# Softmax normalized through the turning product, negated scores with their minimum, and gates of two pairs written together

## The chip, the cores and the metric

The kernel runs on one core of a Trainium2 chip. The metric is the device time of one execution in microseconds, the median of the runs; lower is better. The core has a matmul engine (TensorE, here PE), VectorE (DVE), ScalarE (ACT), GpSimd (POOL) and a queue that issues transfers (SP). Each engine works through its own instructions in the order in which they stand.

## What is computed

Two blocks follow each other on a sequence of 512 positions of width 1024. The first has two layers with feed-forward networks, of which the second holds a sparse attention with 8 heads (`dsa` in the kernel); the second block holds a gated delta rule and a forgetting attention with 16 heads of width 64 (`fox`). Of the reference, the two attentions matter here:

```python
def dsa_attention(q, k, v, qi, ki, wi):            # cut
    ...
        s = jnp.where(valid[:, :, None, None, :], s, -jnp.inf)
        p = jax.nn.softmax(s, axis=-1)
        o = jnp.einsum('btgrk,btkgd->btgrd', p, v_sel.astype(jnp.float32))
...
def forgetting_attention(q, k, v, cum):            # cut
    ...
        logits = jnp.einsum('bqhd,bkhd->bhqk', q_b, k)
        logits = logits + (c_b[..., :, None] - cum_k[..., None, :])
        q_pos = start + jnp.arange(Q_BLOCK)
        mask = key_pos[None, :] <= q_pos[:, None]
        p = jax.nn.softmax(jnp.where(mask, logits, -jnp.inf), axis=-1)
        return jnp.einsum('bhqk,bkhd->bqhd', p, v)
...
    o = forgetting_attention(q, k, v, cum).reshape(B, S, FOX_WIDTH)
    o = o * jax.nn.silu(z.astype(jnp.float32))
```

## The kernel before

Nearly all of the time goes into projections. A weight of 128x1024 is loaded as f32 (`raw`), cast to a high part `wh` on ACT (line 139) and a low part `wl` on DVE or GpSimd (line 140), and each product is made of three matmuls (lines 145 to 147) into a PSUM bank named `acc`, of which there are three. Scores go into two banks `sa`, turned probabilities into two banks `sb`.

**Both attentions** go by steps. In `dsa` a step is a head and a query block `i` of 128 rows: 8 heads times 4 blocks, of widths 128, 256, 384 and 512. In `fox` it is a pair of heads `p`, a head `a` of it and a block `i`: 8 times 2 times 4 = 64 steps of the same widths. A step has three parts, each issued one step after the last:

- `scores`: products into `sa`; one DVE instruction adds a bias, writes the sum to `x` (tile `p`) and its row maximum to `st`; a small DVE instruction makes the maximum negative (lines 897 and 1472); ACT takes the exponential with that as its bias and sums the row (898 and 1473); DVE takes the reciprocal (899 and 1474); `x` is multiplied by it, in `dsa` on ACT (900), in `fox` on DVE (1475).
- `turn`: each of the `i + 1` blocks of 128x128 in `x` is turned by a PE transpose with the identity (lines 907 and 1484), and ACT copies the bank to `pT` (909 and 1485).
- `values`: in `dsa` `i + 1` plain f32 matmuls of 128x128 (line 917); in `fox` once for each pair (line 1493).

Between these parts units of projection work are let in by a generator (`fill`): a unit is one set of three matmuls, or six in `v_units`. In `fox`, `pair_units(p + 1)` brings, while pair `p` is at work, the query and the key of the next pair, and by turns the values or the two gates `z` of two pairs. When a gate's projection ends, ACT applies Silu to its bank (line 1430) and then loads the table set that has exponential and logarithm again (line 126, kept in program order). Query and key are normalized seven units after their projection ends (`normed`): ACT logarithm and exponential (lines 173 and 174) and three DVE steps make `r`, GpSimd multiplies `x` by it (1398), and ACT and DVE cut it into halves (1410 to 1420).

The order in which instructions stand on each engine is not that of the text: a planner sets it when the program is built, from when it thinks each operand is ready. So an edit in one place can move instructions in others.

Of the kernel before, what the change touches and what calls it, by code (L numbers as in the profile page):

```python
# [12 lines left out]
AF = mybir.ActivationFunctionType  # L13
ALU = mybir.AluOpType
# [5 lines left out]
D, S, DFF, KT, P = 1024, 512, 2816, 8, 128  # L20
# [8 lines left out]
def f32(ap):  # L29
    return ap.bitcast(F32)  # L30
# [410 lines left out]
def c4(ap, c):  # L441
    return ap[:, c * P:(c + 1) * P]
# [275 lines left out]
DSA_SCALE = 128.0 ** -0.5  # L718
TAKEN = -3.0e38
# [64 lines left out]
def dsa(self, tables):  # L784
    nc, tc, A = self.nc, self.tc, self.A
    with tc.tile_pool(name="ds", bufs=1) as ds:
        def T(name, shape=(P, S), dtype=F32, bufs=None):
            return ds.tile(list(shape), dtype, name=name, bufs=bufs)
# [26 lines left out]
        ps = self.bank()  # L815
# [21 lines left out]
        pt = self.bank("sb")  # L837
# [17 lines left out]
        bias = [cneg]  # L855
        for i in range(1, 4):
            W = (i + 1) * P
            x = T(f"isc{i}", (P, W))

            for t in range(2):  # L860
# [3 lines left out]
                for a, ps in enumerate(pair):  # L864
                    hh = 2 * t + a
                    r = self.tmp()
# [19 lines left out]
        prob, pos = {}, {}  # L886
        ogh, ogl = T("ogh", (P, KT, S), F32R), T("ogl", (P, KT, S), F32R)

        def scores(h, i):
            W = (i + 1) * P  # L890
            ps = self.bank("sa")
            nc.tensor.matmul(ps[:, :W], c4(qT[h], i), kT[h // 4][:, :W], start=True, stop=True)
            x = T("p", bufs=3)[:, :W]
            st = T("st", (P, 4), bufs=4)
            nc.vector.tensor_tensor_reduce(x, ps[:, :W], bias[i], 1.0, TAKEN, op0=ALU.add, op1=ALU.max,
                                           accum_out=st[:, 0:1])
            nc.vector.tensor_scalar(st[:, 1:2], st[:, 0:1], -DSA_SCALE, None, op0=ALU.mult)
            nc.scalar.activation(x, x, AF.Exp, scale=DSA_SCALE, bias=st[:, 1:2], accum_out=st[:, 2:3])
            nc.vector.reciprocal(st[:, 3:4], st[:, 2:3])
            nc.scalar.activation(x, x, AF.Copy, scale=st[:, 3:4])  # L900
            prob[h, i] = x

        def turn(h, i):
            x, W = prob.pop((h, i)), (i + 1) * P
            pt = self.bank("sb")
            for j in range(i + 1):
                nc.tensor.transpose(c4(pt, j), c4(x, j), self.ident)
            pT = prob[h, i] = T("pT", bufs=3)
            nc.scalar.copy(pT[:, :W], pt[:, :W])

# [20 lines left out]
        for t in range(len(steps) + 3):  # L931
            if t < len(steps):
                while len(qT) <= steps[t][0]:
                    fill.run(1)
                scores(*steps[t])
                if t < 12:
                    for r in range(t * 16 // 12, (t + 1) * 16 // 12):
                        top(3, r)
            if t == 19:
                fill.add(self.out_units(feed, 2, [ogh[:, u] for u in range(4)], [ogl[:, u] for u in range(4)], one))  # L940
            fill.run(3 if t < 5 else 1 if t < 16 else 2)
            if 1 <= t <= len(steps):
                turn(*steps[t - 1])
            if t >= 2 and t - 2 < len(steps):
                values(*steps[t - 2])
# [400 lines left out]
def fox(self, feed, gate, tail):  # L1346
    nc, tc, A = self.nc, self.tc, self.A
    BF = dt.bfloat16
    with tc.tile_pool(name="fx", bufs=1) as fx, tc.tile_pool(name="fxd", bufs=1, space=bass.MemoryType.DRAM) as dr:
        def T(name, shape=(P, S), dtype=F32, bufs=None):  # L1350
            return fx.tile(list(shape), dtype, name=name, bufs=bufs)
# [13 lines left out]
        ps, ps_q, ps_k = [self.bank() for _ in range(3)]  # L1365
# [16 lines left out]
        qs, ks, vs, zs, og = {}, {}, {}, {}, []  # L1382

        def normed(name, dst, p, gain_col, sq_scale, eps, halves):
            def done(ps):
                x, sq, sh = T("x", bufs=2), self.tmp(), T("sqh", dtype=F32R, bufs=2)
                nc.scalar.activation(sq, ps, AF.Square, scale=sq_scale)
                nc.scalar.activation(x, ps, AF.Copy, scale=gain_col)
                nc.scalar.activation(sh, ps, AF.Square, scale=sq_scale)
                sl = T("sql", dtype=F32R, bufs=2)  # L1390
                nc.vector.tensor_sub(sl, sq, f32(sh))

                def stats():
                    pn = self.bank()
                    nc.tensor.matmul(pn, blk, sh, start=True, stop=False)
                    nc.tensor.matmul(pn, blk, sl, start=False, stop=True)
                    r = self.rstd_from(pn, T("r", bufs=2), eps)
                    nc.gpsimd.tensor_mul(x, x, r)  # L1398
                    dst[p] = halves(x)
                fill.later(7, stats)  # L1400
            return done
# [21 lines left out]
        def v_copy(p):  # L1423
            v = vs[p] = vs[p + 1] = T("v", (P, 4, 256), bufs=2)
            return lambda c2, ps: nc.scalar.copy(v[:, 2 * c2:2 * c2 + 2].rearrange("p c d -> p (c d)"), ps)

        def z_done(p):
            def done(ps):
                zs[p] = T("sz", bufs=2)
                nc.scalar.activation(zs[p], ps, AF.Silu)  # L1430
                self.log_exp()
            return done

        def q_done(p):
# [2 lines left out]
        def pair_units(p):  # L1437
            nb = T("ncb", (P, 2, S), bufs=2)
            nc.sync.dma_start(nb.rearrange("p h s -> p (h s)"),
                              cd[2 * p:2 * p + 2].rearrange("h s -> (h s)").rearrange("(o f) -> o f", o=1)  # L1440
                              .to_broadcast([P, 2 * S]))
            nbs[p] = nb
            k_done = normed("k", ks, p, self.prm("b_kn"), 0.125, None, k_halves)
            if p == 0:
                q_done(0)(ps_q)
                k_done(ps_k)
            else:
                if p > 1:
                    yield from self.project_units(feed, q_done(p))
                yield from self.project_units(feed, k_done)  # L1450
            if p % 2 == 0:
                yield from self.v_units(feed, v_copy(p))
            else:
                yield from self.project_units(feed, z_done(p - 1))
                yield from self.project_units(feed, z_done(p))
            if p == 0:
                yield from self.project_units(feed, q_done(1))

        nbs, prob, pTs = {}, {}, {}

        def scores(p, a, i):
            q, (k, kl) = qs[p][:, a], ks[p]
            W = (i + 1) * P
            ps = self.bank("sa")
            nc.tensor.matmul(ps[:, :W], c4(q, i), k[:, a, :W], start=True, stop=False)
            nc.tensor.matmul(ps[:, :W], c4(q, i), kl[:, a, :W], start=False, stop=False)
            nc.tensor.matmul(c4(ps, i), ib, mb, start=False, stop=True)
            x = T("p", bufs=3)[:, :W]
            st = T("st", (P, 4), bufs=4)
            nc.vector.tensor_tensor_reduce(x, ps[:, :W], nbs[p][:, a, :W], 1.0, TAKEN, op0=ALU.add, op1=ALU.max,  # L1470
                                           accum_out=st[:, 0:1])
            nc.vector.tensor_scalar(st[:, 1:2], st[:, 0:1], -1.0, None, op0=ALU.mult)
            nc.scalar.activation(x, x, AF.Exp, bias=st[:, 1:2], accum_out=st[:, 2:3])
            nc.vector.reciprocal(st[:, 3:4], st[:, 2:3])
            nc.vector.tensor_scalar(x, x, st[:, 3:4], None, op0=ALU.mult)
            prob[p, a, i] = x

        def turn(p, a, i):
            if i == 0:
                pTs[p, a] = T("pT", (P, 4, S), bufs=2)  # L1480
            x, W = prob.pop((p, a, i)), (i + 1) * P
            pt = self.bank("sb")
            for j in range(i + 1):
                nc.tensor.transpose(c4(pt, j), c4(x, j), self.ident)  # L1484
            nc.scalar.copy(pTs[p, a][:, :i + 1, i * P:(i + 1) * P], pt[:, :W].rearrange("p (j t) -> p j t", t=P))


# [17 lines left out]
        for t in range(len(steps) + 2):  # L1505
            if t < len(steps):
                p, a, i = steps[t]
# [246 lines left out]
```

## Time and profile before

| | us |
|---|---|
| median of 3 runs (2778.74 to 2782.1) | 2779.63 |
| profiled execution | 2783.07 |
| its span | 2781.3 |
| PE busy in it | 2684.0 |
| DVE busy | 1729.3 |
| ACT busy | 1194.4 |
| POOL busy | 240.4 |

The span runs from the first to the last instruction that the profile shows. The busy share is a mean over stages with different limits, so the stretches that hold the edited lines have to be read by themselves. A row of the timeline joins consecutive instructions of one line; its second number is the time from the start of the first to the end of the last. PE records overlap: the next starts before the last has drained, and the spacing of starts is what a record costs.

### The profile page before, as it was taken

To read this page: it belongs to the slowest core of one execution; us is meant where nothing else is said; L and a number is where in the kernel's file an instruction comes from. 1 tells how busy PE (TensorE), PEld (TensorE's weight loads), DVE (VectorE), ACT (ScalarE), POOL (GpSimd) and SP (SyncE) were. 2 spreads that over 40 slices of the span, in tenths; PEclk is the share of its full clock that TensorE was granted. 3 is DMA by queue.
4 is the path that set the end of the run, shared out by engine and by line. 5 is a ranking of instruction groups with operands and counts; after the bars stand their busy time and mean duration, and the time that the engine had idled before them with its cause. 6 is when DMAs were issued, how large, how long until landed. Compare 5 with 4: busy or idle time off the path is not lost. (4 is left out here: it accounts for less than half of the span.)

```text
span 2781.3 us, 38312 instructions
## 1 busy us (share of the span) xinstructions
PE 2684.0 (97%) x14903; PEld 2192.8 (79%) x14903; DVE 1729.3 (62%) x3065; ACT 1194.4 (43%) x2200; POOL 240.4 (9%) x224
## 2 busy tenths in 40 slices
PE   8999999999999999999899999988999999999998
PEld 6888878788888888887778888876777777777776
DVE  6454576764545644447956444478777777677776
ACT  4232254532323422224364222265655554577774
POOL 0000002000000000003410000021111111120001
PEclk9999999999999999999999999998999999999999
DMA  5343432243443432323213333223333333132221
GB/s 187 117 138 113 121 103 69 84 144 114 136 121 107 136 111 97 93 87 91 69 39 91 99 99 94 83 83 93 101 99 101 111 98 97 48 101 69 76 67 63
DMA packets 106709, 274.60 MB, mean 99 GB/s; under 512 B 35464, under 2 KB 39552, under 8 KB 106528
## 3 DMA queue, kind: packets, MB, share of 16 engines
q1 hardware_dynamic: 106528, 272.15, 32.6%
q8 instruction: 118, 1.93, 0.3%
q14 instruction: 63, 0.52, 0.1%
HBM read 267.79 MB, written 4.31 MB: 98 GB/s over the span
## 5 line engine op out<-in xcount | busy, mean ns | idle before, releaser
L145 PE MATMUL acc<-xh,wh 128*128 128x512 f32 (+2 forms) x2320 | 911.5, 393 | 18.1 <-ACT xh L186 8.4
L146 PE MATMUL acc<-xl,wh 128*128 128x512 f32 (+1 forms) x2320 | 903.9, 390 | 3.3 <-POOL xl L151 2.4
L139 ACT CAST wh<-raw 128x1024 fp32r<-128x1024 f32 (+3 forms) x430 | 439.0, 1021 | 1089.8 <-PE acc L146 716.1
L147 PE MATMUL acc<-xh,wl 128*128 128x512 f32 (+1 forms) x2320 | 899.7, 388 | 2.1 <-DVE wl L140 2.1
L140 DVE TENSOR_TENSOR wl<-raw,wh 128x1024 fp32r<-128x1024 f32 (+2 forms) x410 | 490.4, 1197 | 67.4 <-ACT wh L139 64.7
L145 PEld LDWEIGHTS acc<-xh,wh 128*128 128x128 f32 (+1 forms) x2320 | 437.0, 188 | 109.1 <-ACT xh L186 8.3
L146 PEld LDWEIGHTS acc<-xl,wh 128*128 128x128 f32 x2320 | 436.6, 188 | 92.2 <-issue 3.7
L147 PEld LDWEIGHTS acc<-xh,wl 128*128 128x128 f32 x2320 | 436.1, 188 | 92.6 <-DVE wl L140 4.0
L146 PE MATMUL acc<-al,wh 128*128 128x512 f32 (+1 forms) x720 | 278.2, 386 | 0.0
L147 PE MATMUL acc<-ah,wl 128*128 128x512 f32 (+1 forms) x720 | 277.8, 386 | 0.0
L145 PE MATMUL acc<-ah,wh 128*128 128x512 f32 (+1 forms) x720 | 277.4, 386 | 0.0
L249 DVE SCALAR_TENSOR_TENSOR h<-acc,h 128x512 f32<-128x512 f32 x128 | 88.4, 691 | 214.8 <-PE acc L147 214.4
L289 DVE TENSOR_TENSOR tmp<-acc,rstd 128x512 f32<-128x512 f32 x88 | 60.9, 691 | 239.0 <-PE acc L147 239.0
L287 DVE TENSOR_TENSOR tmp<-acc,rstd 128x512 f32<-128x512 f32 x88 | 60.8, 691 | 175.7 <-PE acc L147 175.6
L146 PEld LDWEIGHTS acc<-al,wh 128*128 128x128 f32 x720 | 135.2, 188 | 28.6 <-DVE al L151 0.8
L145 PEld LDWEIGHTS acc<-ah,wh 128*128 128x128 f32 x720 | 135.2, 188 | 28.2
L147 PEld LDWEIGHTS acc<-ah,wl 128*128 128x128 f32 x720 | 135.2, 188 | 28.0
L140 POOL TENSOR_TENSOR wl<-raw,wh 128x1024 fp32r<-128x1024 f32 (+1 forms) x20 | 47.8, 2390 | 872.5 <-ACT wh L139 861.7
L145 PE MATMUL acc<-ogh,wh 128*128 128x512 f32 (+1 forms) x256 | 105.0, 412 | 10.5 <-DVE h L1301 6.7
L147 PE MATMUL acc<-ogh,wl 128*128 128x512 f32 (+1 forms) x256 | 100.3, 392 | 0.0
L146 PE MATMUL acc<-ogl,wh 128*128 128x512 f32 (+1 forms) x256 | 100.0, 391 | 0.0
L150 ACT CAST ah<-tmp 128x512 fp32r<-128x512 f32 x88 | 54.8, 622 | 64.0 <-DVE tmp L290 64.0
(450 smaller groups left out, 3472.0 us busy)
## 6 DMA issues: line engine op xcount, KB each, us to landing
raw<-in_wi_dram SPq DMA_DIRECT2D x176, 512.0 KB
raw<-in_wo_dram SPq DMA_DIRECT2D x64, 512.0 KB
raw<-in_ada_w_dram SPq DMA_DIRECT2D x48, 512.0 KB
raw<-in_a_in_dram SPq DMA_DIRECT2D x48, 512.0 KB
raw<-in_b_in_dram SPq DMA_DIRECT2D x24, 512.0 KB
raw<-in_wo_dram SPq DMA_DIRECT2D x24, 384.0 KB
raw<-in_a_out_dram SPq DMA_DIRECT2D x16, 512.0 KB
big<-rd SPq DMA_DIRECT2D x13, 512.0 KB
```

The costliest lines, as they stand in the source:

```text
L139: nc.scalar.copy(wh[:, :n], raw[:, :n])
L140: self.lo_eng.tensor_tensor(wl[:, :n], raw[:, :n], f32(wh[:, :n]), op=ALU.subtract)
L145: nc.tensor.matmul(out, ah, bh, start=start, stop=False)
L146: nc.tensor.matmul(out, ah, bl, start=False, stop=False)
L147: nc.tensor.matmul(out, al, bh, start=False, stop=stop)
L150: self.nc.scalar.copy(hi, x)
L249: nc.vector.scalar_tensor_tensor(self.h[m], ps, scale(m), self.h[m], op0=ALU.mult, op1=ALU.add)
L287: nc.vector.tensor_mul(t, pg, rstd)
L289: nc.vector.tensor_mul(u, pu, rstd)
```

## The change

In both attentions the reducing instruction now multiplies by a negative number (-1, in `dsa` the negative scale) and takes the row minimum, which is the bias that the exponential wants; the exponential's scale is -1. The small multiplication is gone. The reciprocal no longer multiplies the probabilities: it multiplies the identity into a tile `dg` of 128x128 (three buffers), on ACT in `dsa` and on DVE in `fox`. The transposes become plain matmuls of the probabilities with `dg`, which turn and scale in one. The gates: the first of two is left in its bank until the second is projected, and both are then written after each other, with one call that loads the other table set. The tile `r` has one buffer in place of two.

```diff
@@ dsa: scores, turn
-            nc.vector.tensor_tensor_reduce(x, ps[:, :W], bias[i], 1.0, TAKEN, op0=ALU.add, op1=ALU.max,
+            nc.vector.tensor_tensor_reduce(x, ps[:, :W], bias[i], -DSA_SCALE, -TAKEN, op0=ALU.add, op1=ALU.min,
                                            accum_out=st[:, 0:1])
-            nc.vector.tensor_scalar(st[:, 1:2], st[:, 0:1], -DSA_SCALE, None, op0=ALU.mult)
-            nc.scalar.activation(x, x, AF.Exp, scale=DSA_SCALE, bias=st[:, 1:2], accum_out=st[:, 2:3])
+            nc.scalar.activation(x, x, AF.Exp, scale=-1.0, bias=st[:, 0:1], accum_out=st[:, 2:3])
             nc.vector.reciprocal(st[:, 3:4], st[:, 2:3])
-            nc.scalar.activation(x, x, AF.Copy, scale=st[:, 3:4])
-            prob[h, i] = x
+            dg = T("dg", (P, P), bufs=3)
+            nc.scalar.activation(dg, self.ident, AF.Copy, scale=st[:, 3:4])
+            prob[h, i] = x, dg
...
-                nc.tensor.transpose(c4(pt, j), c4(x, j), self.ident)
+                nc.tensor.matmul(c4(pt, j), c4(x, j), dg, start=True, stop=True)
@@ fox: normed, z_done
-                    r = self.rstd_from(pn, T("r", bufs=2), eps)
+                    r = self.rstd_from(pn, T("r"), eps)
...
-                zs[p] = T("sz", bufs=2)
-                nc.scalar.activation(zs[p], ps, AF.Silu)
-                self.log_exp()
+                zs[p] = ps
+                if p % 2:
+                    for q in (p - 1, p):
+                        ps, zs[q] = zs[q], T("sz", bufs=2)
+                        nc.scalar.activation(zs[q], ps, AF.Silu)
+                    self.log_exp()
@@ fox: scores, turn
-            nc.vector.tensor_tensor_reduce(x, ps[:, :W], nbs[p][:, a, :W], 1.0, TAKEN, op0=ALU.add, op1=ALU.max,
+            nc.vector.tensor_tensor_reduce(x, ps[:, :W], nbs[p][:, a, :W], -1.0, -TAKEN, op0=ALU.add, op1=ALU.min,
                                            accum_out=st[:, 0:1])
-            nc.vector.tensor_scalar(st[:, 1:2], st[:, 0:1], -1.0, None, op0=ALU.mult)
-            nc.scalar.activation(x, x, AF.Exp, bias=st[:, 1:2], accum_out=st[:, 2:3])
+            nc.scalar.activation(x, x, AF.Exp, scale=-1.0, bias=st[:, 0:1], accum_out=st[:, 2:3])
             nc.vector.reciprocal(st[:, 3:4], st[:, 2:3])
-            nc.vector.tensor_scalar(x, x, st[:, 3:4], None, op0=ALU.mult)
-            prob[p, a, i] = x
+            dg = T("dg", (P, P), bufs=3)
+            nc.vector.tensor_scalar(dg, self.ident, st[:, 3:4], None, op0=ALU.mult)
+            prob[p, a, i] = x, dg
...
-                nc.tensor.transpose(c4(pt, j), c4(x, j), self.ident)
+                nc.tensor.matmul(c4(pt, j), c4(x, j), dg, start=True, stop=True)
```

The planner gives a new order in places. On ACT, in `fox`, where the first of the two gates of pairs 2 and 3 stands (`sz` is the gate, `p` the probabilities, `ks` the key's halves), there stood before:

```order
L1473 ACTIVATE p_21148,st_21149<-p_21148,st_21149 128x256
L173 ACTIVATE r_21164<-acc_21161,eps0_79 128x512
L174 ACTIVATE r_21164<-r_21164,ln_a_87 128x512
L1430 ACT_TABLE_LOAD
L1430 ACTIVATE sz_21188<-acc_21125 128x512
L126 ACT_TABLE_LOAD
L1485 COPY pT_21191<-sb_21192 128x128
L1417 CAST ks_21172<-x_21095 64x512
L1419 CAST ks_21172<-x_21095 64x512
L1417 CAST ks_21172<-x_21095 64x512
L1419 CAST ks_21172<-x_21095 64x512
L1473 ACTIVATE p_21199,st_21200<-p_21199,st_21200 128x384
```

After the two rows of lines 173 and 174 there stand now:

```order
L139 CAST wh_21272<-raw_21271 128x1024
L1491 COPY pT_21187<-sb_21188 128x128
L1435 ACT_TABLE_LOAD
L1435 ACTIVATE sz_21248<-acc_21124 128x512
L1478 ACT_TABLE_LOAD
L1478 ACTIVATE p_21195,st_21196<-p_21195,st_21196 128x384
L1418 CAST ks_21171<-x_21094 64x512
L1420 CAST ks_21171<-x_21094 64x512
L1418 CAST ks_21171<-x_21094 64x512
L1420 CAST ks_21171<-x_21094 64x512
L1491 COPY pT_21187<-sb_21221 128x2x128
L1478 ACTIVATE p_21229,st_21230<-p_21229,st_21230 128x512
```

The first gate still stands by itself, the second a row further on; a weight cast and the 384-wide exponential moved ahead of the key's casts.

On ACT, in `fox`, at the 512-wide step that ends a pair, while values are projected, there stood before:

```order
L1485 COPY pT_21546<-sb_21586 128x2x128
L139 CAST wh_21645<-raw_21644 128x1024
L1425 COPY v_21445<-acc_21561 128x512
L1485 COPY pT_21546<-sb_21626 128x3x128
L139 CAST wh_21731<-raw_21730 128x1024
L1473 ACTIVATE p_21594,st_21595<-p_21594,st_21595 128x512
L1473 ACTIVATE p_21635,st_21636<-p_21635,st_21636 128x128
L1485 COPY pT_21546<-sb_21663 128x4x128
```

and now:

```order
L1491 COPY pT_21544<-sb_21584 128x2x128
L139 CAST wh_21643<-raw_21642 128x1024
L1478 ACTIVATE p_21592,st_21593<-p_21592,st_21593 128x512
L1426 COPY v_21443<-acc_21559 128x512
L1491 COPY pT_21544<-sb_21624 128x3x128
L139 CAST wh_21729<-raw_21728 128x1024
L1478 ACTIVATE p_21633,st_21634<-p_21633,st_21634 128x128
L1491 COPY pT_21544<-sb_21661 128x4x128
```

The 512-wide exponential moved ahead of the copy of `v`, a copy of `pT` and a weight cast.

On PE, in `fox`, at the change from pair 2 to pair 3 (lines 1465 to 1467 are the new pair's first scores, line 1484 turns the last pair's 384-wide step), there stood before:

```order
L147 MATMUL acc_21212<-xh7_104,wl_21121 128x512
L1465 MATMUL sa_21260<-ks_21172,qs_21084 128x128
L1466 MATMUL sa_21260<-kl_21173,qs_21084 128x128
L1467 LDWEIGHTS ib_19897
L1467 MATMUL sa_21260<-mb_19895,ib_19897 128x128
L145 MATMUL acc_21279<-xh0_97,wh_21207 128x512
L146 MATMUL acc_21279<-xl0_105,wh_21207 128x512
L147 MATMUL acc_21279<-xh0_97,wl_21208 128x512
L1484 MATMUL sb_21255<-ident_74,p_21199 128x128 x3
```

and now:

```order
L147 MATMUL acc_21208<-xh7_104,wl_21120 128x512
L1490 MATMUL sb_21253<-dg_21200,p_21195 128x128 x3
L1470 MATMUL sa_21258<-ks_21171,qs_21083 128x128
L1471 MATMUL sa_21258<-kl_21172,qs_21083 128x128
L1472 LDWEIGHTS ib_19897
L1472 MATMUL sa_21258<-mb_19895,ib_19897 128x128
L145 MATMUL acc_21277<-xh0_97,wh_21203 128x512
L146 MATMUL acc_21277<-xl0_105,wh_21203 128x512
L147 MATMUL acc_21277<-xh0_97,wl_21204 128x512
```

The turn moved ahead of the new pair's scores and of three projection matmuls.

## Rows read from the trace of the kernel before

**Rows 1.** Page, part 1: busy us (share of span) and instructions

```profile
PE 2684.0 (97%) x14903; PEld 2192.8 (79%) x14903; DVE 1729.3 (62%) x3065; ACT 1194.4 (43%) x2200; POOL 240.4 (9%) x224
```

**Rows 2.** Stretches: length, busy us of PE, PEld, DVE, ACT, POOL, granted clock, DMA share, GB/s

```profile
1353.00:1402.00 49.00, 38.46 (x185) 29.48 (x183) 46.41 (x133) 21.67 (x55) 18.42 (x10) 0.90 0.18 55
1402.00:1460.00 58.00, 56.83 (x313) 45.26 (x314) 26.53 (x96) 37.72 (x89) 9.66 (x5) 0.97 0.14 44
...
1402.00:1407.00 5.00, 5.00 (x14) 3.01 (x15) 2.82 (x11) 2.88 (x6) 1.27 (x1) 0.66 0.20 78
...
2470.00:2752.00 282.00, 268.15 (x1470) 211.70 (x1470) 199.76 (x481) 201.53 (x385) 23.51 (x15) 0.99 0.23 72
...
2540.00:2544.00 4.00, 4.00 (x13) 2.89 (x13) 0.63 (x3) 0.97 (x4) 0.00 (x0) 0.63 0.36 131
```

**Rows 3.** Groups by line, engine, shape: records, busy us, mean ns, idle before

```profile
L907 PE MATMUL sb<-ident,p 128*128 128x128 f32 x80 | 14.6, 280 | 1.2 <-ACT p L900 1.2
L917 PE MATMUL acc<-pT,v 128*128 128x128 f32 x160 | 24.3, 279 | 0.0
L1484 PE MATMUL sb<-ident,p 128*128 128x128 f32 x160 | 28.6, 277 | 10.8 <-DVE p L1475 8.3 <-DVE st L1472 2.3
```

**Rows 4.** Timeline of PE in `dsa`: start us, us, instruction, how many

```profile
1409.69 0.60 PE L907 MATMUL sb<-ident,p 128*128 128x128 f32 x4
1410.13 0.61 PE L917 MATMUL acc<-pT,v 128*128 128x128 f32 x4
```

**Rows 5.** Groups by line: softmax steps on DVE and ACT, table loads

```profile
L1472 DVE TENSOR_SCALAR st<-st 128x1 f32<-128x1 f32 x64 | 9.5, 148 | 0.8
L1475 DVE TENSOR_SCALAR p<-p,st 128x384 f32<-128x384 f32 x16 | 9.6, 598 | 0.3
L1475 DVE TENSOR_SCALAR p<-p,st 128x512 f32<-128x512 f32 x16 | 7.8, 487 | 0.4
L1475 DVE TENSOR_SCALAR p<-p,st 128x128 f32<-128x128 f32 x16 | 5.4, 337 | 0.2
L900 ACT ACTIVATE p<-p,st 128x512 f32<-128x512 f32 x8 | 5.7, 722 | 0.2 <-DVE st L899 0.2
L900 ACT ACTIVATE p<-p,st 128x128 f32<-128x128 f32 x8 | 3.2, 400 | 1.2 <-DVE st L897 1.0 <-DVE st L899 0.2
L1430 ACT ACT_TABLE_LOAD x8 | 10.3, 1283 | 0.1
```

**Rows 6.** Waits of PE from 2470 to 2752: total us, times, longest

```profile
PE sb L1484 <- DVE p L1475: 8.3, 5, 2.2
PE sb L1484 <- DVE st L1472: 2.3, 4, 1.6
PE sa L1466 <- DVE kl L1420: 2.1, 6, 0.4
```

**Rows 7.** Timeline ahead of the 512-wide turn that ends pair 3

```profile
2604.39 0.69 DVE L1470 CUSTOM_DVE_ANT_0 p<-sa,ncb 128x512 f32<-128x512 f32 x1
...
2605.01 1.22 DVE L140 TENSOR_TENSOR wl<-raw,wh 128x1024 fp32r<-128x1024 f32 x1
...
2605.55 1.06 ACT L139 CAST wh<-raw 128x1024 fp32r<-128x1024 f32 x1
...
2606.49 0.73 ACT L1473 ACTIVATE p<-p,st 128x512 f32<-128x512 f32 x1
...
2608.60 0.63 PE L1484 MATMUL sb<-ident,p 128*128 128x128 f32 x4 [2.15 <-DVE p L1475]
```

**Rows 8.** Timeline at the change from pair 2 to pair 3

```profile
2569.78 0.62 ACT L1473 ACTIVATE p<-p,st 128x384 f32<-128x384 f32 x1
...
2571.37 0.55 PE L1484 MATMUL sb<-ident,p 128*128 128x128 f32 x3 [0.91 <-DVE p L1475]
```

**Rows 9.** Timeline of PE in `dsa` where the search of top entries ends

```profile
1401.91 0.70 PE L892 MATMUL sa<-kT,qT 128*128 128x512 f32 x1 [2.19 <-DVE st L895]
```

More of the change, by code (lines that the diff above doesn't have):

```diff
@@ L894, in scores @@
             st = T("st", (P, 4), bufs=4)
-            nc.vector.tensor_tensor_reduce(x, ps[:, :W], bias[i], 1.0, TAKEN, op0=ALU.add, op1=ALU.max,
+            nc.vector.tensor_tensor_reduce(x, ps[:, :W], bias[i], -DSA_SCALE, -TAKEN, op0=ALU.add, op1=ALU.min,
                                            accum_out=st[:, 0:1])
-            nc.vector.tensor_scalar(st[:, 1:2], st[:, 0:1], -DSA_SCALE, None, op0=ALU.mult)
-            nc.scalar.activation(x, x, AF.Exp, scale=DSA_SCALE, bias=st[:, 1:2], accum_out=st[:, 2:3])
+            nc.scalar.activation(x, x, AF.Exp, scale=-1.0, bias=st[:, 0:1], accum_out=st[:, 2:3])
             nc.vector.reciprocal(st[:, 3:4], st[:, 2:3])
-            nc.scalar.activation(x, x, AF.Copy, scale=st[:, 3:4])
-            prob[h, i] = x
+            dg = T("dg", (P, P), bufs=3)
+            nc.scalar.activation(dg, self.ident, AF.Copy, scale=st[:, 3:4])
+            prob[h, i] = x, dg
         def turn(h, i):
-            x, W = prob.pop((h, i)), (i + 1) * P
+            (x, dg), W = prob.pop((h, i)), (i + 1) * P
             pt = self.bank("sb")
             for j in range(i + 1):
-                nc.tensor.transpose(c4(pt, j), c4(x, j), self.ident)
+                nc.tensor.matmul(c4(pt, j), c4(x, j), dg, start=True, stop=True)
             pT = prob[h, i] = T("pT", bufs=3)
@@ L1480, in turn @@
                 pTs[p, a] = T("pT", (P, 4, S), bufs=2)
-            x, W = prob.pop((p, a, i)), (i + 1) * P
+            (x, dg), W = prob.pop((p, a, i)), (i + 1) * P
             pt = self.bank("sb")
             for j in range(i + 1):
-                nc.tensor.transpose(c4(pt, j), c4(x, j), self.ident)
+                nc.tensor.matmul(c4(pt, j), c4(x, j), dg, start=True, stop=True)
             nc.scalar.copy(pTs[p, a][:, :i + 1, i * P:(i + 1) * P], pt[:, :W].rearrange("p (j t) -> p j t", t=P))
```

## Prediction

> **What bounds the kernel now.** I read the busy line of the page first: the matmul engine (PE) is busy for 2684.0 us of a span of 2781.3 [rows 1]. A kernel so full of PE work gains little from work taken off VectorE (DVE) or ScalarE (ACT), and pays for nearly everything that is put on PE. So the question is what the edits put on PE and how much PE idles where they stand. The busy time by stretch answers the second part [rows 2]. The attention of `dsa` falls into two pieces: until 1402 us PE is busy for 38.46 of 49 us and DVE for 46.41, because DVE searches the top entries there; from 1402 to 1460 PE is busy for 56.83 of 58. In `fox`, from 2470 to 2752, PE is busy for 268.15 of 282 us, DVE for 199.76 and ACT for 201.53. PE sets the time in `fox` and in the second piece of `dsa`, with an idle remainder of 13.85 and 1.17 us.
>
> **The turning product.** This is the term that decides. Before, a block of 128x128 probabilities is turned by a transpose on PE; after, by a plain matmul of two f32 tiles with the scaled identity as the moving operand. The kernel before has both kinds, of the same shape and type. Line 907 turns 10 blocks for each of 8 heads, 80 in all, and has 80 matmul records of 280 ns [rows 3]. Line 917 multiplies 10 blocks for each of 8 heads by plain f32 matmuls, 80 in all, and has 160 records of 279 ns: each plain product is two passes, each transpose one [rows 3]. Spacing is read from two neighbouring runs of the timeline [rows 4]: four transposes in a row span 0.60 us, so one takes (0.60 - 0.28) / 3 = 0.11 us after its neighbour; four records of line 917, two products, span 0.61. A plain product thus costs 0.22 us of PE against 0.11. The change turns 80 blocks in `dsa` and 160 in `fox` [rows 3]: 80 x 0.11 = 8.8 us and 160 x 0.11 = 17.6 us more on PE, 26.4 in all. Weight loads differ too, but the spacing of line 917 already contains them.
>
> The Trainium skill, FP8 and Floating Point Precision, section TensorE Precision Notes, says that true FP32 takes four passes through the array and makes no exception for turning. By that rule transpose and product would cost the same and this term would be 0; the records and the spacing above contradict it, and a rival below takes it up.
>
> **Removed from DVE and ACT.** The minimum of the negated scores makes the small multiplication needless: 64 x 148 ns = 9.5 us off DVE in `fox` [rows 5], and the same for 32 steps in `dsa`, 4.7 at that price. Scaling the identity in place of the probabilities takes the 128-wide time for every width: on DVE in `fox` 337 ns in place of 337, 598 and 487 at widths 128, 384 and 512, [rows 5], between 0 and 0.26 us a step and some 7 us over 64; on ACT in `dsa` 400 ns in place of up to 722. The reducing instruction keeps its form and only its constants change: nothing. None of these is PE time. They help where PE waits for the softmax, and there alone.
>
> **Waits of PE in `fox`.** The list of waits gives 8.3, 2.3 and 2.1 us for its main ones [rows 6]. One pattern comes at 2538.8, 2608.6 and 2676.9 us: PE waits 2.15 us for the last 512-wide block row of a pair [rows 7]. The reduction starts at 2604.39, a `wl` subtraction of 1.22 us then holds DVE ahead of the small multiplication, the exponential starts only at 2606.49 behind an ACT cast that started at 2605.55, and PE starts at 2608.60. After the change the exponential needs no multiplication, and the order puts it ahead of the `v` copy, a `pT` copy and that cast. It can start at about 2605.2 and end with its readout at 2606.1 (0.73 + 0.2); the `wl` subtraction is left until 2606.3; reciprocal and scaled identity (0.16 + 0.34) end near 2606.9. PE starts 1.7 us earlier, less 0.2 because the turn now stands ahead of two score matmuls: 1.5 us each, 4.5 in all.
>
> At the change of a pair the 384-wide exponential ran after four `ks` casts, and PE waited until 2571.37 [rows 8]. The order now puts this exponential ahead of the casts and the turn ahead of the new pair's scores. But a weight cast goes ahead of them too, so the casts and the scores behind them come about 1.3 us later. What the turn gains the scores lose. I count 0.5 us each, 1.5 for three. One stretch partly at the lower clock (1.2 GHz), 0.63 granted over 4 us right after the wait that ends at 2538.8 [rows 2], costs 4 x 0.37 = 1.5 us; if the wait shrinks it goes. The sum for `fox` is 17.6 - 4.5 - 1.5 - 1.5 = +10.1. Its bounds are +17.6, when no wait shrinks, and 17.6 - 13.85 - 1.5 = +2.3, when all do.
>
> **`dsa`.** 24 of the 80 blocks are turned before 1402 us, 56 after it. In the first piece PE comes 24 x 0.11 = 2.6 us later to the wait of 2.19 us at 1401.91, which ends when DVE has taken a score bank [rows 9]; DVE comes there 12 x 0.148 = 1.8 us earlier. So the wait is gone. The granted clock of 0.66 in the 5 us behind it [rows 2], mostly the lower level, goes with it, 5 x 0.34 = 1.7. In the second piece PE has next to no idle time and pays 56 x 0.11 = 6.2. Sum: 8.8 - 2.2 - 1.7 = +4.9, between +8.8 and +8.8 - 2.2 - 1.7 - 1.2 = +3.7.
>
> **The gates.** The text makes two gates together; the order does not. In the rows of ACT the first gate stands almost where it was, an exponential and four casts stand between it and the second, and each still has its table load before and after it. Counted over `fox`, 18 loads become 16: 2 x 1.28 = 2.6 us of ACT [rows 5], which PE does not wait for by name. The first gate's read frees its score bank about 1.5 us later, ahead of the next use: nothing. **The single buffer of `r`** makes a logarithm wait for GpSimd's product of the norm before. Within the loop these are some 8 us apart; at the start of `fox` they are neighbours, and the keys come about 2 us later, against scores that start only after 16 more units of work: 0, at most 1 us.
>
> **Sum.** 10.1 + 4.9 = +15.0 us. The profiled execution took 2783.07 us with a span of 2781.3 and gives 2798.1; it lies 3.4 above the median of 2779.63, and I forecast against the median: **2794.6 us**.
>
> **Rivals.** (a) The waits stay, because other work takes the place of what is removed: the full price, +26.4, 2806.0. For it: DVE and ACT stay above 70% in `fox`, and the weight casts were moved among the softmax's steps. Against it: the steps ahead of the 2.15 us waits are shorter and earlier in the order. (b) Every idle microsecond is used up: 2.3 + 3.7 = +6, 2785.6; with `dsa` left without cost it is 2782. For it: DVE and ACT have less to do in every step while PE has more. Against it: 0.5 us waits stand between steps that the change leaves alone (the halves of the keys). (c) Faster: the plain product costs what the transpose does, one pass, as the rule of equal passes would have it. Then only the relief is left, -(4.5 + 1.5 + 1.5) - (2.2 + 1.7) = -11.4, 2768.2. It decides from an extra PE price of 7.5 + 3.9 = 11.4 us over 240 blocks, 48 ns a block; line 917 shows 110. (d) New waits: a product now needs two results from two engines, and the moved casts delay weights; with one wait of 2.15 us more for each of seven changes of pair it is 26.4 + 15 = +41, 2821.
>
> **How the numbers follow.** Forecast, between +8 and +21: 0.68. (a), up to +27: 0.12. (b): 0.10. (c): 0.04. (d): 0.06. The range goes from (b) at 2784 to (a) at 2806 and leaves out (c), (d) and the edges, some 0.13. A measurement of this kernel can tell about 0.2%, 5.6 us, from no change. Slower by more than that, over 2785.2: forecast, (a), (d) and a little of (b), 0.88. Within it: most of (b), 0.08. Faster: (c), 0.04.
>
> **What would show it.** In the profile after, the turning lines (1490 in `fox`) should have 320 matmul records where 160 stood, the `dsa` ones 160 for 80, with the spacing of 0.11 us; the wait at the 512-wide turn should be under 1 us; the lower clock near 1402 should be gone; 16 table loads should remain in `fox`. I am wrong if the turning lines keep 160 and 80 records, or if `fox` takes less than 282 us from its first score to its last value.

## The result, and the profile after

The changed kernel took 2798.26 us (median of 5 runs, 2790.97 to 2805.11) against 2779.63; the ratio is 1.0056, 95% interval 1.0042 to 1.0071. It is slower, as forecast, and the median lies 3.7 us over the forecast of 2794.6. But its runs spread over 14 us, those of the kernel before over 5, and the cost does not sit where the prediction had put it.

The busy line of the page after, and the packets of the queue that carries PE's instructions (packets, MB, share), after and then before:

```profile
PE 2702.7 (97%) x15143; PEld 2222.1 (80%) x15143; DVE 1709.2 (61%) x2969; ACT 1190.8 (43%) x2198; POOL 242.0 (9%) x224
...
q8 instruction: 120, 1.97, 0.3%
```

```profile
q8 instruction: 118, 1.93, 0.3%
```

PE has 240 matmul records more and 18.7 us more of busy time [rows 1], and the span (2792.0) grew by 10.7. DVE lost 20.1 us of work and ACT 3.6. The groups of the turning lines after, `dsa` first, and the scaled identity:

```profile
L908 PE MATMUL sb<-dg,p 128*128 128x128 f32 x160 | 24.0, 281 | 8.2 <-ACT dg L901 8.2
...
L1490 PE MATMUL sb<-dg,p 128*128 128x128 f32 x320 | 46.7, 277 | 2.0 <-DVE dg L1481 2.0
...
L1481 DVE TENSOR_SCALAR dg<-ident,st 128x128 f32<-128x128 f32 x64 | 18.7, 294 | 1.8
```

The 80 and 160 records of [rows 3] became 160 and 320 of the same duration: two passes a block, as predicted. The waits before them in `fox` fell from 10.8 to 2.0 us.

Where the time went is read from four marks, the starts of the first score and of the last value matmul of each attention. In the answers by line they are the first and last start of a group (the numbers ahead are the shortest, middle and longest duration in ns). Before:

```profile
L892 PE MATMUL sa<-kT,qT x64: 272/484/1061, 1353.2 to 1450.8; 128*128 128x128 f32 x16, 128*128 128x256 f32 x16, 128*128 128x384 f32 x16, 128*128 128x512 f32 x16
L917 PE MATMUL acc<-pT,v x160: 270/275/421, 1371.6 to 1458.9; 128*128 128x128 f32 x160
L1465 PE MATMUL sa<-ks,qs x64: 220/379/497, 2476.3 to 2744.3; 128*128 128x128 f32 x16, 128*128 128x256 f32 x16, 128*128 128x384 f32 x16, 128*128 128x512 f32 x16
L1493 PE MATMUL mg<-pT,v x128: 272/432/644, 2507.6 to 2752.9; 128*64 128x512 f32 x32, 128*64 128x384 f32 x32, 128*64 128x256 f32 x32, 128*64 128x128 f32 x32
```

After:

```profile
L892 PE MATMUL sa<-kT,qT x64: 272/454/595, 1354.5 to 1455.2; 128*128 128x128 f32 x16, 128*128 128x256 f32 x16, 128*128 128x384 f32 x16, 128*128 128x512 f32 x16
L918 PE MATMUL acc<-pT,v x160: 270/275/318, 1373.0 to 1464.2; 128*128 128x128 f32 x160
L1470 PE MATMUL sa<-ks,qs x64: 220/392/476, 2484.1 to 2754.3; 128*128 128x128 f32 x16, 128*128 128x256 f32 x16, 128*128 128x384 f32 x16, 128*128 128x512 f32 x16
L1499 PE MATMUL mg<-pT,v x128: 272/432/643, 2520.5 to 2763.6; 128*64 128x512 f32 x32, 128*64 128x384 f32 x32, 128*64 128x256 f32 x32, 128*64 128x128 f32 x32
```

So `dsa` took 1458.9 - 1353.2 = 105.7 us before and 109.7 after (+4.0), `fox` 276.6 and 279.5 (+2.9), and the stage between them, which the change does not touch, 1017.4 and 1019.9 (+2.5). The rest is +1.3 ahead of `dsa`, within what single executions differ by there. The table gives the same lengths, read in the same way, for every profile of this study (the last column is the median of the timed runs and the ratio to the kernel before, with its 95% interval):

| kernel | ahead | `dsa` | between | `fox` | median us; ratio |
|---|---|---|---|---|---|
| before | 1353.2 | 105.7 | 1017.4 | 276.6 | 2779.63 |
| after | 1354.5 | 109.7 | 1019.9 | 279.5 | 2798.26; 1.0056 (1.0042 to 1.0071) |
| e1 after again | 1354.6 | 110.0 | 1025.0 | 281.3 | 2801.82; 1.0069 (1.0056 to 1.0082) |
| e2 plain products only | 1355.3 | 110.5 | 1025.8 | 284.4 | 2805.45; 1.0081 (1.0067 to 1.0095) |
| e3 all but the product | 1353.5 | 106.4 | 1012.2 | 270.1 | 2774.87; 0.9975 (0.9965 to 0.9985) |
| e4 `dsa` as before | 1355.8 | 106.0 | 1017.3 | 279.5 | 2787.80; 1.0012 (1.0001 to 1.0023) |
| e5 after, 96 instructions put in | 1356.1 | 109.3 | 1012.7 | 279.9 | 2791.26; 1.0033 (1.0021 to 1.0044) |
| e6 as e3, 160 put in | 1360.6 | 106.4 | 1024.4 | 271.5 | 2793.18; 1.0039 (1.0025 to 1.0052) |
| e7 negated minimum only | 1354.5 | 103.9 | 1017.2 | 272.7 | 2778.62; 0.9992 (0.9983 to 1.0001) |
| e8 product and `r` only | 1355.8 | 110.4 | 1028.8 | 285.6 | 2810.57; 1.0102 (1.0088 to 1.0115) |
| e9 gates and `r` only | 1354.4 | 105.8 | 1017.2 | 280.4 | 2783.34; 1.0009 (1.0000 to 1.0018) |
| e10 as e3, again | 1354.9 | 103.9 | 1015.5 | 270.1 | 2774.54; 0.9979 (0.9970 to 0.9989) |

What became of PE's time in `fox` is read in the same stretch, from the first score to the last value matmul (length, busy us of PE, PEld, DVE, ACT, POOL, granted clock, DMA share, GB/s), for before, after, e2, e3, e8 and e9:

```profile
2476.30:2752.90 276.60, 262.75 (x1445) 206.87 (x1443) 194.59 (x476) 196.85 (x378) 22.32 (x14) 0.99 0.23 71
2484.10:2763.60 279.50, 275.16 (x1604) 225.60 (x1603) 180.86 (x413) 196.66 (x378) 23.70 (x14) 1.00 0.23 70
2491.50:2775.90 284.40, 278.42 (x1604) 226.69 (x1603) 196.13 (x476) 196.87 (x377) 23.67 (x14) 0.99 0.23 69
2472.20:2742.30 270.10, 260.37 (x1445) 204.59 (x1443) 188.08 (x414) 195.58 (x378) 23.35 (x14) 1.00 0.24 73
2495.00:2780.60 285.60, 278.07 (x1604) 226.54 (x1603) 190.99 (x478) 197.96 (x380) 23.66 (x14) 0.99 0.23 69
2477.40:2757.80 280.40, 264.90 (x1445) 209.00 (x1443) 198.37 (x477) 196.51 (x379) 22.32 (x14) 0.98 0.22 70
```

Length less busy time is what PE idles: 13.85 us before, 4.34 after, 5.98 in e2, 9.73 in e3, 7.53 in e8, 15.50 in e9.

Now the stretches that answer [rows 2] (length, busy us of PE, PEld, DVE, ACT, POOL, granted clock, DMA share, GB/s): all of `fox`, `fox` without its first pair and a half, and the second piece of `dsa`:

```profile
2477.80:2763.00 285.20, 280.86 (x1633) 230.60 (x1632) 185.24 (x419) 200.10 (x383) 25.83 (x15) 1.00 0.23 71
2545.00:2763.00 218.00, 217.64 (x1261) 178.06 (x1260) 140.76 (x319) 151.13 (x290) 16.84 (x10) 1.00 0.23 71
1403.00:1465.00 62.00, 60.35 (x366) 51.14 (x365) 22.16 (x68) 33.28 (x83) 9.90 (x6) 1.00 0.14 43
```

From 2545 us on PE idles for 0.36 of 218 us: nothing is left to wait for. The stretches of lower clock that followed the waits of before, at 1402 and at 2540, are gone; both stretches have a granted clock of 1.00. The waits of PE in `fox` after, against [rows 6], all fall into the first pair and a half:

```profile
PE sb L1490 <- DVE dg L1481: 2.0, 2, 1.0
PE sa L1470 <- DVE st L1476: 2.0, 1, 2.0
PE sa L1471 <- DVE kl L1421: 0.4, 2, 0.2
```

And the place of [rows 7] after the change:

```profile
2615.15 0.69 DVE L1476 CUSTOM_DVE_ANT_0 p<-sa,ncb 128x512 f32<-128x512 f32 x1
...
2615.77 1.22 DVE L140 TENSOR_TENSOR wl<-raw,wh 128x1024 fp32r<-128x1024 f32 x1
...
2615.89 0.72 ACT L1478 ACTIVATE p<-p,st 128x512 f32<-128x512 f32 x1 [0.34 <-DVE st L1476]
...
2617.10 0.29 DVE L1481 TENSOR_SCALAR dg<-ident,st 128x128 f32<-128x128 f32 x1
...
2617.84 1.05 PE L1490 MATMUL sb<-dg,p 128*128 128x128 f32 x8
```

The exponential starts 0.74 us after the reduction in place of 2.10, beside the `wl` subtraction and no longer behind it; the scaled identity is done at 2617.39, and PE comes at 2617.84, without a wait.

### The profile page after: what moved, and what is told of

Same layout as the page of the kernel before. It is cut to its first block, busy times and chain, and to the rows that moved or that the text cites. A ratio compares the mean times of both kernels' runs of the same rounds, so it can differ in the third digit from the quotient of the medians.

```text
span 2792.0 us, 38759 instructions
## 1 busy us (share of the span) xinstructions
PE 2702.7 (97%) x15143; PEld 2222.1 (80%) x15143; DVE 1709.2 (61%) x2969; ACT 1190.8 (43%) x2198; POOL 242.0 (9%) x224
```

## Experiments

**The changed kernel again (e1).** No edit.

> The changed kernel once more, unaltered, for a second profile and five more times. Theory A (the cost of the change sits in the two attentions: +4.0 us in dsa and +2.9 in fox, by the progress of the projection matmuls in the two profiles, and the rest of the difference is stretches of lower clock that fall differently in each execution): the second profile again shows about +4 across dsa and +3 across fox, and the rest of the excess over before lies in stages that the change does not touch. Theory B (the whole +15.6 us belongs to the two attentions and the first profile caught a lucky execution): the second profile shows 10 us or more across fox and dsa. Both expect a median of 2791 to 2800 us.

`dsa` +4.3, `fox` +4.7 (a stretch of lower clock lies in it), the stage between +7.6. The attentions stay near +7 to +9; most of the rest sits in code that the change leaves alone. As to the place theory A holds; but what it put the rest down to, stretches of lower clock alone, leaves out a pause, and the median of 2801.82 lies just over the range that both theories gave. In that stage PE stops in the middle of 64 like matmuls, the fourth of the eight groups that line 1173 makes in the kernel's small triangular solves. The timeline of PE, first of this run, then of the first profile after, then of the kernel before:

```profile
2105.49 0.64 PE L1173 MATMUL mg<-uc,z 32*32 32x16 f32 x55
...
2111.33 0.34 PE L1173 MATMUL mg<-uc,z 32*32 32x16 f32 x9 [5.19 <-issue]
```

```profile
2105.54 0.64 PE L1173 MATMUL mg<-uc,z 32*32 32x16 f32 x55
...
2109.28 0.26 PE L1173 MATMUL mg<-uc,z 32*32 32x16 f32 x9 [3.10 <-issue]
```

```profile
2100.85 0.73 PE L1172 MATMUL mg<-uc,z 32*32 32x16 f32 x64
```

"issue" means that no releaser is seen. The 64 matmuls read slices of the same two tiles, so that data should hold the 56th alone is unlikely. The pause has the same place in both executions and another length. A second one, of about 1 us, stands some 130 us later, after the 56th matmul of the sixth group.

**The price of the product by itself (e2).** Both turning lines of the kernel before:

```diff
-                nc.tensor.transpose(c4(pt, j), c4(x, j), self.ident)
+                nc.tensor.matmul(c4(pt, j), c4(x, j), self.ident, start=True, stop=True)
```

> The kernel before, with the 240 transposes made plain matmuls with the plain identity; probabilities are normalized as before, all other work is as before. Only the PE price of the turning product. Theory A (PE price of 0.11 us a block, filled partly into waits that are elastic): PE busy rises by 20 to 27 us, fox and dsa get 10 to 20 us longer, 2790 to 2800 us. Theory B (the waits are held by the softmax chain on DVE and ACT, which this run leaves as it was, so nothing is absorbed): +26, about 2806. If a plain product costs what a transpose does: 2780.

By the time (2805.45) it looks like B, by the stages it is A: `fox` is only 7.8 us longer where PE's busy time grew by 15.7 (262.75 to 278.42), `dsa` 4.8, and 8.4 of the excess is the stage between, with a pause of the same kind (5.00 us). The waits of PE in `fox`, with the softmax chain as long as before:

```profile
PE sb L1484 <- DVE p L1475: 3.8, 5, 2.3
PE sa L1466 <- DVE kl L1420: 1.6, 4, 0.4
PE acc L1395 <- ACT sqh L1389: 0.6, 1, 0.6
```

The waits at the turn fell from 10.6 [rows 6] to 3.8 us, and all idle time of PE from 13.85 to 5.98, with nothing made shorter. PE took a part of its extra work into them.

**All but the product (e3, and again e10).** The changed kernel with the two normalizations and transposes of before; in `dsa`, and alike in `fox`:

```diff
-            dg = T("dg", (P, P), bufs=3)
-            nc.scalar.activation(dg, self.ident, AF.Copy, scale=st[:, 3:4])
-            prob[h, i] = x, dg
+            nc.scalar.activation(x, x, AF.Copy, scale=st[:, 3:4])
+            prob[h, i] = x
...
-                nc.tensor.matmul(c4(pt, j), c4(x, j), dg, start=True, stop=True)
+                nc.tensor.transpose(c4(pt, j), c4(x, j), self.ident)
```

> The changed kernel without the turning product: negated scores and their minimum, gates and the single buffer of r as in the change; probabilities are normalized and turned by transposes as before. Theory A (the shorter chain from scores to exponential takes away most of the 13.9 us that PE idles in fox): 4 to 9 us faster than before, 2771 to 2776, and waits of PE on the turn in fox fall from 10.6 to under 4 us. Theory B (the waits went because PE has more work, not because the chain is shorter): within 2 us of before, and the 2.15 us waits at the 512-wide turn remain.

> The kernel of e3 unaltered, for a second profile and a second verdict: all of the change but the turning product. If e3 is faster than the kernel before, 2771 to 2778 and a ratio of 0.996 to 0.999; in fox 5 to 7 us shorter than before and no pause in the gated delta rule. If the first profile was a lucky one: within 0.1% of before.

Both are faster than the kernel before: 2774.87 and 2774.54, ratios 0.9975 and 0.9979, both intervals below 1. `fox` is 6.5 us shorter in both profiles. This version beats both kernels. The waits of PE in `fox` in e3:

```profile
PE sb L1485 <- DVE p L1476: 5.2, 9, 1.2
PE sa L1467 <- DVE st L1472: 2.3, 1, 2.3
PE sa L1468 <- DVE kl L1419: 2.0, 6, 0.4
```

The longest wait at the turn fell to 1.2 us, but their sum stays at 5.2, over the 4 that theory A set: the shorter chain removes about half, not all. The idle time as a whole fell by 4.1 us (13.85 to 9.73); most of the other 2.4 us is the lower clock of before [rows 2], which is gone (1.00 over the stretch).

**`dsa` as before (e4).** The edits of `fox`, the gates and `r` stay; `scores` and `turn` of `dsa` are those of the kernel before.

> The changed kernel with dsa as before; only fox and its gates are changed. Theory A (dsa costs 4.0, fox 2.9): 4 us less than the changed kernel, +3 over before plus what the clock does; across dsa the progress equals before within 1 us, across fox +3. Theory B (the first profile caught a lucky fox): fox +10 and the time within 5 us of the changed kernel.

`dsa` 106.0, `fox` 279.5, as in the first profile after: +2.9 is the price of the change in `fox`. The stage between is at 1017.3, as before, and PE's pause is not among its waits. Giving back `dsa` took 10 to 14 us off the changed kernel (2798.26 and 2801.82 to 2787.80), of which only 4 were ever in `dsa`: the others came back where no line differs. Neither theory has the time: theory A gave 4 us less and +3 over before, measured are +5.6 over its own runs of before (2782.22); theory B gave within 5 us of the changed kernel.

**Where a block of instructions ends (e5, e6).** The packets of the instruction queue show 1.93 MB in 118, 16.4 KB each. The changed kernel's trace has 15143 matmuls of PE, as many weight loads and 452 other instructions; over them the 120 packets make 64 bytes an instruction, 256 instructions to a packet. Two kernels shift the instructions of PE without touching what follows, by transposes of 4 columns at the start; e5 is the changed kernel with 48, e6 is e3 with 80:

```diff
         s.setup(ctx)
+        pad = s.bank("sb")
+        for _ in range(48):
+            nc.tensor.transpose(pad[:, 0:4], s.ones_d[0:4, :], s.ident[:4, :4])
```

> The changed kernel with 48 transposes of 4 columns (a weight load and a matmul each, 96 instructions of PE) put in at its start, whose results nothing reads. In the changed kernel the 80 turned blocks of dsa stand for 160 more PE instructions ahead of the gated delta rule, which the change does not touch; 160 and 96 make 256, and the transfers of PE instructions in the trace are 16384 bytes each. Theory C (the pause of 3.1 to 5.2 us in the middle of 64 like matmuls in the gated delta rule, at about 2105 us, is PE waiting for its next block of instructions, and the change only moved the end of a block there): the pause is gone, the stage from 1834 to 2442 us of before takes within 2 us of before instead of 2.5 and 8.3 more, and the median falls by 3 to 8 us in spite of some 3 us for the padding, to 2792 to 2798, with less scatter. Theory D (the pause is data or chance): it stays, and the median is 2802 to 2805.

> The kernel of e3 (all of the change but the turning product) with 80 such transposes at its start: 160 PE instructions, as many as the turning product adds in dsa, and no other edit. Theory C: the pause of 3 us or more appears in the middle of the 64 like matmuls of the gated delta rule, the stage takes 5 to 10 us longer than in e3, and the time is 8 to 15 us over e3 (some 5 us of it the padding), 2783 to 2790. Theory D: no pause; 2778 to 2780.

The same matmuls on the timeline of PE, e5 and then e6:

```profile
2105.59 0.73 PE L1172 MATMUL mg<-uc,z 32*32 32x16 f32 x64
```

```profile
2107.03 0.64 PE L1171 MATMUL mg<-uc,z 32*32 32x16 f32 x54
...
2110.57 0.39 PE L1171 MATMUL mg<-uc,z 32*32 32x16 f32 x10 [2.90 <-issue]
```

In e5 the pause is gone, the stage takes 1012.7 us in place of 1019.9 and 1025.0, and the median falls by 7 to 10.6 us, to just under the range of theory C, although the padding spans 5.3 us of PE at the start (`ahead` grew by 1.6). In e6 the pause appears in a kernel that never had it, and the stage takes 12.2 us more than in e3; that and the time, 18.3 over e3 with a padding that spans 8.7, lie over the ranges given. As to the pause theory C holds in both directions: it comes and goes with the number of PE instructions ahead of that place.

The profile names no releaser, but the trace's DMA records do. In every profile with the pause one packet of 16384 bytes of the instruction queue lands during it, and PE goes on 1.35 to 1.52 us after the packet's end (start us; the clock is that granted in the 10 us from the packet's start):

| kernel | pause us | packet from, to | PE goes on | after the packet | clock |
|---|---|---|---|---|---|
| after | 3.10 | 2106.92, 2107.88 | 2109.28 | 1.40 | 0.83 |
| e1 | 5.19 | 2108.93, 2109.90 | 2111.33 | 1.43 | 0.54 |
| e2 | 5.00 | 2108.75, 2109.71 | 2111.16 | 1.45 | 0.53 |
| e6 | 2.90 | 2108.18, 2109.22 | 2110.57 | 1.35 | 0.55 |
| e8 | 3.44 | 2110.65, 2111.60 | 2113.12 | 1.52 | 0.54 |
| before, line 1193 | 0.59 | 2104.00, 2104.95 | 2106.41 | 1.46 | 1.00 |

The last row is a short pause of the kernel before. It stands 80 weight loads, 79 matmuls and a semaphore instruction further on than the place of the long one, 160 in all, and that is where the end of a packet should lie when 160 instructions ahead are missing. So PE waits there for its next instructions; e5 has the packet and the places of before, and PE goes through both without a stop. In the changed kernel PE goes through the 125 matmuls that end at the pause, nearly all of them small, in 2.2 us (2103.99 to 2106.18). Why the packet comes no sooner is not shown.

The pause is only a part of what it goes with. The clock of the 10 us from the packet's start, for after, e1 and e5 (busy columns as before, the clock is the third number from the end):

```profile
2106.92:2116.92 10.00, 7.64 (x116) 6.57 (x117) 3.35 (x10) 5.82 (x17) 0.00 (x0) 0.83 0.03 9
2108.93:2118.93 10.00, 7.60 (x100) 6.25 (x101) 3.23 (x9) 4.73 (x14) 0.00 (x0) 0.54 0.01 3
2107.96:2117.96 10.00, 9.96 (x126) 8.66 (x121) 4.85 (x10) 9.22 (x25) 1.47 (x2) 1.00 0.01 3
```

At 0.54, mostly the lower level of 1.2 GHz, these 10 us lose some 4.6 us (an estimate, 10 x 0.46), about as much as the pause itself; in the first profile after it is 1.7. With the longer pause this makes the stage 7.6 us longer in e1 and only 2.5 in the first profile.

**The negated minimum alone (e7).** The two reductions and exponentials as in the change, nothing else.

> The kernel before with negated scores and their minimum alone (no small multiplication; gates, r, normalization and transposes as before). Theory A (the shorter chain makes the gain of e3): 4 to 7 us faster than before, 2774 to 2778, with fox 4 to 7 us shorter. Theory E (the gain of e3 came from the order of the gates): within 2 us of before.

`fox` is 3.9 us shorter, just under theory A's 4 to 7; the median is 3.1 below its own runs of before (2781.71), but the interval reaches 1.0001. So the minimum makes more than half of e3's gain in `fox` and not all of it, and its effect on the time is not clear of the noise.

**Product and `r` alone (e8).** The scaled identity and the product as in the change; maximum, small multiplication and gates as before.

> The kernel before with the turning product on the scaled identity, and the single buffer of r that makes room for it; the maximum, the small multiplication and the gates are as before. Against e2 it has the shorter scaling (128 columns in place of up to 512) and the same PE price. Theory A: fox 4 to 8 us longer than before and 0 to 3 less than in e2, dsa +4 to +6, the gated delta rule with its pause as in e2: 2800 to 2806.

`fox` is 9.0 us longer, 1.2 more than in e2 and not less, `dsa` +4.7, and the stage between is the longest of all, with its pause. 2810.57 lies over the range given. Scaling the identity in place of the probabilities, cheaper on DVE, left the waits at the turn as they were (3.5 us against 3.8 in e2), and a wait of 2.3 us at the third score of `fox` is new. The first of these lines is of e8, the second of e9:

```profile
PE sa L1466 <- DVE st L1471: 2.3, 1, 2.3
PE sa L1468 <- DVE st L1473: 2.0, 1, 2.0
```

This wait of 2.0 to 2.3 us stands in every profile with the single buffer of `r` and in none of those without it (before, e2, e7). In `fox` the parts add up: +9.0 from e8 and -6.5 from e3 give +2.5, and the change has +2.9; but both parts hold that wait, so the closeness is in part chance.

**Gates and `r` alone (e9).** `z_done` and the buffer of `r` as in the change.

> The kernel before with the gates of two pairs written together and the single buffer of r, and nothing else. In fox, e3 was 6.4 us shorter than before by the progress of the projection matmuls, the negated minimum alone (e7) 3.9. Theory F (effects in fox add up): the gates and r are worth the rest, fox 1.5 to 3.5 us shorter, 2776 to 2780. Theory G (the gates stay apart in the order, so they do nothing, and the rest was a stretch of lower clock): fox within 1 us of before, 2779 to 2783.

`fox` is 3.8 us longer and not shorter: theory F falls. Theory G's 1 us does not hold by this profile either. But the profiled execution (2787.94) lies 4.6 us over the median of its runs, and its granted clock over `fox` is 0.98 against 0.99 before, which by an estimate (280 x 0.01) is some 3 us; the idle time grew by 1.65 us, with the new wait of 2.0 in it. The median (2783.34 against 2781.16) and the interval from 1.0000 leave the whole near nothing. What is left open is why e3 and e10 have 2.6 us less in `fox` than e7, where the same gates come on top of the minimum; I did not separate `r` from the gates.

## Why the prediction was right, and where it was wrong

- **The turning product costs two passes.** Right: 160 and 320 records at 281 and 277 ns. Both profiles and e2 show it, and the rule of equal passes, rival (c), is out.
- **`dsa` +4.9.** Right in size: +4.0 and +4.3. The wait of [rows 9] and the lower clock behind it went as forecast (no wait at 1402, a clock of 1.00 behind it).
- **`fox` +10.1.** The step that failed; it took +2.9. The prediction's own sign of being wrong, under 282 us from the first score to the last value, came true with 279.5. The waits were listed one by one, and each was given what the shorter chain would take from it: 6.0 us of waits and 1.5 of lower clock. The idle time fell by 9.5 us instead (13.85 to 4.34). The run of e2 shows what was left out: PE's own new work flows into those waits, because PE arrives later at each of them while DVE and ACT go on. There the busy time grew by 15.7 us and the idle time fell by 7.9, before any softmax step was shortened. The rest of the miss is in the price: of the 17.6 us only some 14 show, 12.4 as growth of the busy time and about 1.5 that the lower clock gave back; where the other 3.7 went is not shown. The +2.9 is close to the bound of +2.3 that rival (b) had, but not by its mechanism: 4.3 us of idle time were left.
- **What made up for it.** The pause in the gated delta rule was in no term. With the lower clock behind it it is +2.5 and +7.6 us in the two profiles of the stage between and, by e5, at least 7 to 10 us of the median. Without it the changed kernel would have come out at 2786 to 2790 (an estimate: e5's median less the 5.3 us that its padding spans, or the 1.6 by which `ahead` grew), below the forecast and near rival (b). So the right total was luck: it was put together from a term mis-sized by 7 us and one that was missing.
- **The gates do not come together.** Right: the order kept them apart, and e9, which also has the single buffer of `r`, found next to nothing.
- **`r` with one buffer: 0, at most 1 us.** Doubtful. The first scores of `fox` do not come later by more than the stages before account for. But PE then waits 2.0 to 2.3 us for the third score in every profile with the single buffer, and not in before, e2 and e7. e8 and e9 have it without each other's edits, so it goes with `r`; whether the buffer itself or the new order that comes with it makes the wait is not shown.

## To carry to other kernels

A transpose of f32 on PE takes half the passes of a plain f32 product of the same block; using the product to scale as well pays only where the time saved elsewhere is on the path. When work is added to an engine that bounds a stage, reckon first that a part of its idle time there will go into the price (here 8 to 10 of 14 us), and go wait by wait only after that. And a change in the number of an engine's instructions can move a pause into code far behind it: when a stage that no edit touches gets slower, look for a pause in a run of like instructions, ask the DMA records whether a packet of instructions lands in it, and shift the instructions to test it.

## What was not expected of the hardware

PE stopped for 2.9 to 5.2 us between two of 64 like small matmuls, after the 55th or the 54th, until 1.4 to 1.5 us after a packet of 16384 bytes of instructions had landed. 160 PE instructions more ahead of the place brought the pause (after, e1, e2, e8, e6); 96 more on top of these, 256 in all, took it away (e5), and kernels without additions ahead of it have at most the 0.59 us of before (before, e3, e4, e7, e9, e10). In four of the five profiles the granted clock behind the pause was 0.53 to 0.55 for 10 us, in the fifth 0.83. With the pause the stage takes 1019.9 to 1028.8 us, without it 1012.2 to 1017.4. The pause does not explain how far the runs of one kernel lie apart: e1, with it, spreads over 4.3 us, and e4, without it, over 12.
